# Delta blocks laid out row first and loaded in 12 transfers a group, output weights emitted with the last score row, a shared closing addition

## The chip, the cores and the metric

The kernel runs on one core of a Trainium2 chip. The core has a matrix engine (TensorE, PE in the profile; its weight loads are PEld), a vector engine (DVE), an activation engine (ACT), a general engine (GpSimd, POOL) and a sync engine (SP) that here mostly issues DMAs. Each works through its own instructions in order; semaphores tie them together. The metric is the device time of one execution in microseconds (us).

## The reference

One layer of a hybrid encoder in float32, 1024 positions, width 1024. Cut to what matters:

```python
u = rms_norm(h, mix_norm_gain)
proj = u @ w_in                                   # q,k,v of attention; q,k,v, gate, decay, beta of the delta rule
o_att = rms_norm(chunked_rel_attention(aq, ak, av), att_out_gain)      # own chunk of 64 + 8 chunks back, 8 heads
dq, dk, dv = split(causal_short_conv(dqkv), 3)    # convolution of 4 taps, then silu
o_dn = rms_norm(gated_delta_rule(dq, dk, dv, log_decay, beta), dn_out_gain) * silu(dgate)    # 4 heads of 128
h = h + concat([o_att, o_dn]) @ w_out
h = h + square(relu(rms_norm(h, ffn_norm_gain) @ w_ff1)) @ w_ff2       # 1024 -> 4096 -> 1024
```

Inside the delta rule each chunk and head needs a triangular solve:

```python
a_strict = where(strict, einsum('bhnid,bhnjd->bhnij', k_beta, k) * l_mask, 0.0)
t_mat = a_strict + eye(CHUNK)
value = triangular_solve(t_mat, v_beta, lower=True, unit_diagonal=True)
k_cumdecay = triangular_solve(t_mat, k_beta * exp(decay)[..., None], lower=True, unit_diagonal=True)
```

## The kernel before

Everything is kept feature first, so products contract over the 128 partitions. Each float32 operand is split into a high half (a cast on ACT, line 203) and a low half (a subtraction, line 204), and a product is three matrix multiplications (`mm3`, line 222): hi·lo, hi·hi, lo·hi. A scheduler lays out the instructions of each engine when the program is built, from the order in which the code emits them, their dependencies and its own model of costs; `high_priority` lifts a piece ahead.

The stages:
1. Norm and input projections (`aq_ps`, `ak_ps`, `av_ps`, `dq_ps`, `dv_ps`, `g_ps`).
2. In the shadow of the projections, `delta_prep`: for each of 8 chunks of 128 rows and 4 heads it makes the strictly lower matrix A, 128x128, and stores it to `a_dr` in DRAM (line 577). The 32x32 diagonal blocks of all chunks and heads, 128 of them, are loaded one to a partition (`ad`, line 587), inverted by 31 steps on DVE (lines 595 and 596) into `xd`, transposed back into `ad`, and both are stored as `x_dr` and `y_dr` (line 604).
3. `delta_low(b)`, once for each of two groups of four chunks: it loads the inverted blocks into `l_w` (line 630, from `y_dr`), and the blocks `l_xa` (line 633 from `x_dr`, line 634 from `a_dr`), then joins them by 32x32 matrix products into `l_p` (lines 640 and 649) to inverses of 64x64. `delta_merge` (line 658) joins these to 128x128, with `m_sa` and `m_yb`, just before a chunk needs them.
4. Attention and the delta recurrence, interleaved by a planner that keeps a clock of engines and PSUM banks: score rows `t_sa`, `t_sb` (line 925), softmax pieces `t_pa`, `t_pb` (DVE lines 945 and 956, ACT lines 964 and 968), flips (transposes) on PE into `t_tpa`, `t_tpb` (lines 985 and 1001) with copies to `t_ta`, `t_tb`, values `t_o` (line 1024), and the outputs `mixa` and `mixd` (attention half and delta half). The names with `c_` belong to the delta recurrence (`c_att`, `c_po`, `c_pq`).
5. `out_proj`: `weights(j)` loads eight 128x512 pieces of the output weights (`wo_4` to `wo_7`, then `wo_0` to `wo_3`) through `load_w`, where `wr`, the landing place, has three slots. The low half goes to POOL and DVE by turns. `mixed(hf)` splits the outputs into `mh` and `ml`, and `rows` multiplies: `op` tiles of 128x512, 24 products each. The first of these rows are emitted between the last flips of attention, three `op` tiles side by side; each adds the residual into `h` (DVE, line 1223).
6. The feed-forward, seven products a step after Strassen and Winograd (`q` tiles at line 1343, `p` tiles at line 1439). After the last product the partial results `y` are merged, subtracted from (line 1566) and stored: `y[5]` through ACT's queue (line 1464), `y[4]` through SP's (line 1567).

All DMAs of stages 2 to 4 that the change touches are issued by SP, one after another. PSUM has 8 banks; the mixer's pools hold 3 (`ps_a`, projections), 2 (`ps_t`), 1 (`ps_o`) and 2 (`ps_d`, delta) in that order, and the feed-forward opens its own four tiles of two banks over all of them.

Of the kernel before, what the change touches and what calls it, by code (L numbers as in the profile page):

```python
# [43 lines left out]
NV = 6  # L44
# [54 lines left out]
def hymba_kernel(  # L99
# [31 lines left out]
    mpool = mixer.enter_context(tc.tile_pool(name="mpool", bufs=1))  # L131
    ps_a = mixer.enter_context(tc.tile_pool(name="ps_a", bufs=3, space=PS))
    ps_t = mixer.enter_context(tc.tile_pool(name="ps_t", bufs=2, space=PS))
    ps_o = mixer.enter_context(tc.tile_pool(name="ps_o", bufs=1, space=PS))
    ps_d = mixer.enter_context(tc.tile_pool(name="ps_d", bufs=2, space=PS))

    def page(tag, name, dt=F32, w=512):
# [69 lines left out]

    def load_w(src, name, tags=("wh", "wl")):
        raw = page("wr", name + "_r")
        nc.sync.dma_start(out=raw, in_=src)  # L210
        hi = page(tags[0], name + "_h", F32R)
        lo = page(tags[1], name + "_l", F32R)
        lo_turn[0] += 1
        split(raw, hi, lo, nc.scalar, nc.gpsimd if lo_turn[0] % 2 else nc.vector)
        return hi, lo
# [77 lines left out]
    dg_dr = dram.tile([NT, P, 4, P], F32, name="dg_dr")  # L293
    a_dr = dram.tile([NT, P, 512], F32, name="a_dr")
    x_dr = dram.tile([NT * 4, 32, 4, 32], F32, name="x_dr")
    y_dr = dram.tile([NT * 4, 32, 4, 32], F32, name="y_dr")
    kt_dr = dram.tile([NT, P, 512], F32, name="kt_dr")
# [248 lines left out]
    def delta_prep(kT, ab):  # L546
# [4 lines left out]
        for c in range(NT):  # L551
            n = f"d{c}"
            h4 = slice(4 * c, 4 * c + 4)
            tp = bank(ps_d, n + "_tp")
            four_t(tp, head(kT[c]))
            ss = sumsq(page("pp", n + "_sq"), "p", tp, n)
            if c + 1 < NT:
                kt = page("pp", n + "_kt")
                nc.vector.tensor_tensor(b4(kt), b4(tp), bc_row(ab["edec"][:, 1, h4]), ALU.mult)
                nc.sync.dma_start(out=kt_dr[c], in_=kt)  # L560
            yield 500
            L = decay("pp", n + "_L", ab, h4, tri_s, tri_ur, nc.vector)
            r = rsqrt("p", ss, 4, 1.0, EPS, n)
            br, br2 = ab["br"][:, h4], ab["br2"][:, h4]
            nc.gpsimd.tensor_tensor(br, ab["beta"][:, h4], r, ALU.mult)
            nc.gpsimd.tensor_tensor(br2, br, r, ALU.mult)
            nc.gpsimd.tensor_tensor(ab["nbr"][:, h4], br2, ab["ned"][:, h4], ALU.mult)
            yield 500
            mp = bank(ps_d, n + "_m")
            four(mp, lambda h, hs: kT[c][:, hs], lambda h, hs: kT[c][:, hs])  # L570
            A = page("pp", n + "_A")
            for h in range(4):
                hs = slice(h * P, (h + 1) * P)
                nc.vector.scalar_tensor_tensor(
                    A[:, hs], mp[:, hs], ab["br2"][:, 4 * c + h:4 * c + h + 1], L[:, hs],
                    ALU.mult, ALU.mult)
            nc.sync.dma_start(out=a_dr[c], in_=A)
            yield 900
# [3 lines left out]
        td = page("pp", "td")  # L582
        for c in range(NT):
            for b in range(4):
                bs = slice(32 * b, 32 * b + 32)
                p0 = 16 * c + 4 * b
                nc.sync.dma_start(out=ad[p0:p0 + 4],
                                  in_=a_dr[c].rearrange("r (h e) -> h r e", h=4)[:, bs, bs])
        nc.gpsimd.memset(xf, 0.0)
# [12 lines left out]
        for dst, src in ((x_dr, xd), (y_dr, ad)):  # L602
            for h in range(4):
                nc.sync.dma_start(out=dst[:, :, h, :], in_=src.rearrange("(q h) r e -> h q r e", h=4)[h])

# [11 lines left out]
    def delta_low(b, W, tag):  # L617
# [5 lines left out]
        Y = [w.rearrange("p (c h e) -> p c h e", c=2, h=4) for w in W[-2:]]  # L623
        a4 = a_dr[4 * b:4 * b + 4].rearrange("c r (h e) -> c r h e", h=4)
        for i in range(2):
            nc.gpsimd.memset(W[-2 + i], 0.0)
        for c in range(4):
            q = 16 * b + 4 * c
            for k in range(4):
                nc.sync.dma_start(out=Y[c // 2][32 * k:32 * k + 32, c % 2, :, 32 * (k % 2):32 * (k % 2) + 32],  # L630
                                  in_=y_dr[q + k])
            for r0 in (0, 64):
                nc.sync.dma_start(out=XA[r0:r0 + 32, c], in_=x_dr[q + r0 // 32])
                nc.sync.dma_start(out=XA[r0 + 32:r0 + 64, c], in_=a4[c, r0 + 32:r0 + 64, :, r0:r0 + 32])
        yield clock.now + 8000, "d"
# [22 lines left out]
    def delta_merge(c, W, res):  # L658
# [5 lines left out]
        Yd = W[c // 2].rearrange("p (c h e) -> p c h e", c=2, h=4)[:, c % 2]  # L664
        nc.sync.dma_start(out=A[64:128], in_=a_dr[c].rearrange("r (h e) -> r h e", h=4)[64:128, :, 0:64])
        nc.gpsimd.memset(Y[64:128, :, 0:64], 0.0)
# [161 lines left out]

    def attention(after, delta, values, outputs):

# [266 lines left out]
        while True:  # L1097
# [69 lines left out]
            elif k == "score":  # L1167
                g, t, pp = units[begun]
                score(g, t, pp)
                begun += 1  # L1170
                if pp and begun + 2 < len(units):
                    start(*units[begun + 2][0:2])
                if pp and not g:
                    load_rest(t + 1)
            elif k == "values":
                if next(values, None) is None:
                    values_left = False
                else:
# [7 lines left out]
    def out_proj(result):


        order = (4, 5, 6, 7, 0, 1, 2, 3)
        w, parts, R, begun = [], [], {}, []  # L1190

        def weights(j):
            w.append([None] * NKT)
            for k in order:
                w[j][k] = load_w(w_out[k * P:(k + 1) * P, j * 512:(j + 1) * 512], f"wo{j}_{k}",
                                 (("wh", "u"), ("u", "wl"))[j])

# [217 lines left out]
    def ff2(psw, pools):  # L1415
# [52 lines left out]
        for kb in range(nb):  # L1468
# [198 lines left out]
```

## Time and profile before

| | |
|---|---|
| median of 3 runs | 1276.42 us (1275.62 to 1279.3) |
| profiled execution | 1273.11 us, span 1271.0 us |
| mean granted clock of PE over the span | 0.995 |
| busy: PE, DVE, ACT, POOL | 1241.2, 926.5, 547.6, 289.8 us |

The span is what the profiler saw from the first instruction to the last. In lines of the timeline the columns are the start in us, the length in us, the engine, the line of the code, the operation, what it writes and reads, how many instructions are put together, and, in brackets, how long the engine had been idle before it and what released it (`issue` where the profile names nothing). `SPq` and `ACTq` are the DMA-issuing parts of SP and ACT. In a table of windows the columns are length, busy time of PE, PEld, DVE, ACT and POOL with counts, the clock granted to PE as a share of full speed, the busy share of the core's 16 DMA engines, and what they moved in GB/s.

### The profile page before, as it was taken

To read this page: it belongs to the slowest core of one execution; us is meant where nothing else is said; L and a number is where in the kernel's file an instruction comes from. 1 tells how busy PE (TensorE), PEld (TensorE's weight loads), DVE (VectorE), ACT (ScalarE), POOL (GpSimd) and SP (SyncE) were. 2 spreads that over 40 slices of the span, in tenths; PEclk is the share of its full clock that TensorE was granted. 3 is DMA by queue.
4 is the path that set the end of the run, shared out by engine and by line. 5 is a ranking of instruction groups with operands and counts; after the bars stand their busy time and mean duration, and the time that the engine had idled before them with its cause. 6 is when DMAs were issued, how large, how long until landed. Compare 5 with 4: busy or idle time off the path is not lost.

```text
span 1271.0 us, 18018 instructions
## 1 busy us (share of the span) xinstructions
PE 1241.2 (98%) x6686; PEld 1033.3 (81%) x6686; DVE 926.5 (73%) x1388; ACT 547.6 (43%) x899; POOL 289.8 (23%) x487
## 2 busy tenths in 40 slices
PE   9999999999998999889999999999999999999998
PEld 8778878778888898778878788888887888888886
DVE  7899987654236577774349777677669997997988
ACT  7323132232245665654445454544445543333331
POOL 4425461344132345543210000000000000000034
PEclk9999999999999999989999999999999999999999
DMA  7214353564585532134441333332259623332002
GB/s 226 67 42 139 101 157 107 121 162 118 175 245 150 162 109 71 40 109 133 141 141 67 116 133 117 132 100 96 86 199 368 211 83 112 121 100 94 7 34 99
DMA packets 135398, 158.53 MB, mean 125 GB/s; under 512 B 31760, under 2 KB 79376, under 8 KB 134800
## 3 DMA queue, kind: packets, MB, share of 16 engines
q1 hardware_dynamic: 117216, 135.11, 35.0%
q10 hardware_dynamic: 18096, 22.29, 5.2%
q8 instruction: 52, 0.85, 0.3%
q14 instruction: 34, 0.28, 0.1%
HBM read 109.91 MB, written 47.45 MB: 124 GB/s over the span
## 4 chain that ended last, share of the span: by engine, by line
PE 51%; DVE 8%; issue 2%; ACT 1%; POOLq 1%; POOL 0%; DVEq 0%; ACTq 0%
PE p L1439 21%; PE q L1343 20%; PE op L222 6%; PE t_o L1024 1%; POOLq L1662 1%; DVE ml L204 1%; DVE h L1285 1%; DVE y L1511 0%; PE t_sa L925 0%; DVE q_0a_l L204 0%; DVE y L1507 0%; PE t_tpb L985 0%; DVE p43b_l L204 0%; DVE p73b_l L204 0%; DVE p43a_l L204 0%
## 5 line engine op out<-in xcount | busy, mean ns | idle before, releaser
L1511 POOL TENSOR_TENSOR y<-y,y 128x1024 f32<-128x1024 f32 x6 | 19.3, 3242 | 590.5 <-DVE y L1507 571.6
L1507 DVE TENSOR_TENSOR y<-y,p 128x1024 f32<-128x1024 f32 x46 | 55.1, 1216 | 5.4 <-PE p L1439 4.5
L222 PE MATMUL op<-mh,wo_l 128*128 128x512 f32 x128 | 50.1, 399 | 1.1 <-POOL wo_l L204 1.1
L222 PE MATMUL op<-mh,wo_h 128*128 128x512 f32 x128 | 50.6, 398 | 0.1
L222 PE MATMUL op<-ml,wo_h 128*128 128x512 f32 x128 | 50.2, 395 | 0.0
L945 DVE CUSTOM_DVE_ANT_0 t_pb<-t_sb,biasn 128x256 f32<-128x256 f32 (+1 forms) x64 | 23.2, 401 | 29.8 <-PE t_sb L925 29.8
L964 ACT ACTIVATE t_pb<-t_pb,t_nm 128x256 f32<-128x256 f32 (+1 forms) x64 | 31.4, 491 | 18.1 <-DVE t_nm L956 16.7
L1223 DVE TENSOR_TENSOR h<-op,op_x 128x512 f32<-128x512 f32 x16 | 10.8, 687 | 28.8 <-PE op L222 28.8
L1230 POOL TENSOR_TENSOR op_q<-op_q 128x512 f32<-128x512 f32 x14 | 19.6, 1397 | 47.3 <-ACT op_q L1229 47.2
L222 PEld LDWEIGHTS op<-mh,wo_l 128*128 128x128 f32 x128 | 24.4, 191 | 6.9 <-POOL wo_l L204 1.5
L222 PEld LDWEIGHTS op<-mh,wo_h 128*128 128x128 f32 x128 | 24.4, 191 | 5.9 <-issue 0.5
L222 PEld LDWEIGHTS op<-ml,wo_h 128*128 128x128 f32 x128 | 24.4, 190 | 5.2
L956 DVE CUSTOM_DVE_ANT_0 t_pa<-t_sa,biaso,t_nm 128x384 f32<-128x384 f32 (+2 forms) x48 | 25.0, 543 | 2.3 <-PE t_sa L925 2.0
L222 PE MATMUL g_ps<-uh,wg_h 128*128 128x512 f32 x64 | 25.3, 396 | 1.2 <-ACT wg_h L203 1.2
L968 ACT ACTIVATE t_pa<-t_pa,t_nm 128x384 f32<-128x384 f32 (+2 forms) x48 | 26.4, 550 | 0.0
L222 PE MATMUL aq_ps<-waq_h,uh 128*128 128x512 f32 x64 | 25.4, 400 | 0.8 <-ACT waq_h L203 0.8
L925 PE MATMUL t_sb<-ks,t_q 128*128 128x256 f32 (+1 forms) x144 | 24.0, 294 | 1.7 <-DVE t_nm L945 1.3
L222 PE MATMUL g_ps<-uh,wg_l 128*128 128x512 f32 x64 | 25.2, 393 | 0.4 <-POOL wg_l L204 0.4
L222 PE MATMUL dq_ps<-uh,wdq_h 128*128 128x512 f32 x64 | 25.5, 398 | 0.0
L222 PE MATMUL dv_ps<-uh,wdv_l 128*128 128x512 f32 x64 | 25.4, 397 | 0.0
L222 PE MATMUL dq_ps<-ul,wdq_h 128*128 128x512 f32 x64 | 25.3, 395 | 0.0
L222 PE MATMUL av_ps<-wav_l,uh 128*128 128x512 f32 x64 | 25.2, 394 | 0.0
(1109 smaller groups left out, 4306.7 us busy)
## 6 DMA issues: line engine op xcount, KB each, us to landing
wa<-in_w_ff_dram SPq DMA_DIRECT2D x32, 512.0 KB
a<-in_w_ff_dram SPq DMA_DIRECT2D x32, 512.0 KB
b<-f_dr SPq DMA_DIRECT2D x32, 512.0 KB
f_dr<-yy ACTq DMA_DIRECT2D x16, 512.0 KB
t_q<-q_dr SPq DMA_DIRECT2D x30, 256.0 KB
f_dr<-zz ACTq DMA_DIRECT2D x13, 512.0 KB
ks<-k_dr SPq DMA_DIRECT2D x16, 256.0 KB
wo_r<-in_w_out_dram SPq DMA_DIRECT2D x16, 256.0 KB
```

What stands on the lines that cost most here:

```text
L204: return a.ins, lo_eng.tensor_tensor(lo, src, hi.bitcast(F32), ALU.subtract).ins
L222: nc.tensor.matmul(ps, a, b, start=(first and i == 0), stop=(last and i == n - 1))
L925: nc.tensor.matmul(o, q[m][:, i * P:(i + 1) * P], k[:, c], start=(m == 0), stop=(m == 1))
L945: nc.vector.tensor_tensor_reduce(sb[:, c], bk[:, c], new[g][pp][:, c], -1.0, 3.0e38, ALU.add, ALU.min, nm[:, 4 + i:5 + i])
L956: nc.vector.tensor_tensor_reduce(sa[e][:, 0:wa], bk[:, 0:wa], old[g][i][:, 384 - wa:384], -1.0, nm[:, 4 + i:5 + i], ALU.add, ALU.min, nm[: ...
L964: nc.scalar.activation(sb[:, c], sb[:, c], AF.Exp, bias=m, scale=-1.0, accum_out=T["sums"][:, 4 + i:5 + i])
L968: nc.scalar.activation(sa[e][:, 0:wa], sa[e][:, 0:wa], AF.Exp, bias=m, scale=-1.0, accum_out=T["sums"][:, i:i + 1])
L1230: nc.gpsimd.tensor_tensor(acc, acc, sq, ALU.add)
L1343: nc.tensor.matmul(part(ps, q), l[:, s], r, start=(k + m == 0), stop=(k == 3 and m == 2))
L1439: nc.tensor.matmul(part(ps[q], 0) if by_rows else part(ps[q // 2], q % 2), l[:, s], part(r, k), start=(i + k + m == 0), stop=(i + k + m == 4))
L1507: nc.vector.tensor_tensor(y[i][m], y[i][m], ps[m], op)
L1511: eng.tensor_tensor(y[i][m], y[i][m], y[z][m], ALU.add)
```

## The change

Four edits in one:
1. `a_dr`, `x_dr` and `y_dr` lie with the row first in DRAM, then chunk, head and column. So one DMA can take 32 rows of several chunks at once: the loads of the diagonal blocks are 16 (two chunks each) and not 32, and a group of `delta_low` loads by 12 DMAs (two from `x_dr`, two from `a_dr`, eight from `y_dr`) and not 32, for the same bytes. Blocks now stand on partition 32·b + 4·c + h.
2. The first half of the output weights is emitted, with high priority, as soon as the last score row has been emitted, and not when the output projection begins; and all sixteen low halves of output weights are made by DVE.
3. The PSUM pool `ps_a` is made last, so the pools lie in other banks.
4. Of the closing addition `y[5] += y[7]`, one half stays on POOL, the other goes to DVE.

```diff
-    ps_a = mixer.enter_context(tc.tile_pool(name="ps_a", bufs=3, space=PS))
     ps_t = ...
     ps_o = ...
     ps_d = ...
+    ps_a = mixer.enter_context(tc.tile_pool(name="ps_a", bufs=3, space=PS))
...
-    def load_w(src, name, tags=("wh", "wl")):
+    def load_w(src, name, tags=("wh", "wl"), low=None):
...
-        split(raw, hi, lo, nc.scalar, nc.gpsimd if lo_turn[0] % 2 else nc.vector)
+        split(raw, hi, lo, nc.scalar, low or (nc.gpsimd if lo_turn[0] % 2 else nc.vector))
...
-    a_dr = dram.tile([NT, P, 512], F32, name="a_dr")
-    x_dr = dram.tile([NT * 4, 32, 4, 32], F32, name="x_dr")
-    y_dr = dram.tile([NT * 4, 32, 4, 32], F32, name="y_dr")
+    a_dr = dram.tile([P, NT, 512], F32, name="a_dr")
+    x_dr = dram.tile([32, NT * 4, 4, 32], F32, name="x_dr")
+    y_dr = dram.tile([32, NT * 4, 4, 32], F32, name="y_dr")
...
-        for c in range(NT):
+        for c in range(0, NT, 2):
             for b in range(4):
                 bs = slice(32 * b, 32 * b + 32)
-                p0 = 16 * c + 4 * b
-                nc.sync.dma_start(out=ad[p0:p0 + 4],
-                                  in_=a_dr[c].rearrange("r (h e) -> h r e", h=4)[:, bs, bs])
+                p0 = 4 * (NT * b + c)
+                nc.sync.dma_start(out=ad[p0:p0 + 8],
+                                  in_=a_dr[:, c:c + 2].rearrange("r c (h e) -> (c h) r e", h=4)[:, bs, bs])
...
         for dst, src in ((x_dr, xd), (y_dr, ad)):
-            for h in range(4):
-                nc.sync.dma_start(out=dst[:, :, h, :], in_=src.rearrange("(q h) r e -> h q r e", h=4)[h])
+            for p0 in range(0, P, 32):
+                nc.sync.dma_start(out=dst.rearrange("r q h e -> (q h) r e")[p0:p0 + 32], in_=src[p0:p0 + 32])
...
-        for c in range(4):
-            q = 16 * b + 4 * c
+        for r in range(2):
+            q = 2 * r * NT + 4 * b
+            nc.sync.dma_start(out=XA[64 * r:64 * r + 32], in_=x_dr[:, q:q + 4])
+            nc.sync.dma_start(out=XA[64 * r + 32:64 * r + 64],
+                              in_=a4[64 * r + 32:64 * r + 64, :, :, 64 * r:64 * r + 32])
+        for i in range(2):
             for k in range(4):
-                nc.sync.dma_start(out=Y[c // 2][32 * k:32 * k + 32, c % 2, :, 32 * (k % 2):32 * (k % 2) + 32],
-                                  in_=y_dr[q + k])
-            for r0 in (0, 64):
-                nc.sync.dma_start(out=XA[r0:r0 + 32, c], in_=x_dr[q + r0 // 32])
-                nc.sync.dma_start(out=XA[r0 + 32:r0 + 64, c], in_=a4[c, r0 + 32:r0 + 64, :, r0:r0 + 32])
+                q = k * NT + 4 * b + 2 * i
+                nc.sync.dma_start(out=Y[i][32 * k:32 * k + 32, :, :, 32 * (k % 2):32 * (k % 2) + 32],
+                                  in_=y_dr[:, q:q + 2])
...
                 begun += 1
+                if begun == len(units):
+                    with tc.high_priority():
+                        weights()
...
-                merge(nc.gpsimd, 5, 7)
+                for m, eng in enumerate((nc.gpsimd, nc.vector)):
+                    eng.tensor_tensor(y[5][m], y[5][m], y[7][m], ALU.add)
```

The order of the instructions as built shows what moves. SP's queue, the loads of the second group (`l_w` and `l_xa`), among loads for attention (`t_q`, `ks`, `vt`) and recurrence (`c_...`). Before, the last stretch of it:

```order
L665 DMA m_sa<-a_dr 64x4x64
L210 DMA wo_4_r<-in_w_out_dram 128x512
L700 DMA c_jq<-dq_dr 128x512
L210 DMA wo_5_r<-in_w_out_dram 128x512
L210 DMA wo_6_r<-in_w_out_dram 128x512
L905 DMA t_q<-q_dr 64x2x512 x2
L633 DMA l_xa<-x_dr 32x128
L634 DMA l_xa<-a_dr 32x4x32
L858 DMA ks_3991<-k_dr 128x512
L858 DMA ks_3993<-k_dr 128x512
L633 DMA l_xa<-x_dr 32x128
L703 DMA c_kt<-kt_dr 128x512
```

After, the same place:

```order
L635 DMA l_w_4199<-y_dr 32x8x32 x4
L667 DMA m_sa<-a_dr 64x4x64
L907 DMA t_q<-q_dr 64x2x512
L210 DMA wo_6_r<-in_w_out_dram 128x512
L907 DMA t_q<-q_dr 64x2x512
L702 DMA c_jq<-dq_dr 128x512
L907 DMA t_q<-q_dr 64x2x512 x2
L629 DMA l_xa<-x_dr 32x512
L630 DMA l_xa<-a_dr 32x16x32
L860 DMA ks_3955<-k_dr 128x512
L860 DMA ks_3957<-k_dr 128x512
L629 DMA l_xa<-x_dr 32x512
```

Before, 13 more loads of `l_xa` follow the last row shown; after, only `c_kt` and one load of `l_xa` from `a_dr`. Ahead of it 16 loads of `l_w` have become 8.

DVE at the start of the output projection, from the last softmax piece on (`wo_k_l` are low halves of weights, `ml` low halves of the mixed outputs). Before:

```order
L956 ISA t_nm 128x1
L807 SCALAR_TENSOR_TENSOR mixd_6009<-c_tpo,dng,c_jg 128x4x128
L780 TENSOR_TENSOR c_att<-c_mt,c_Lt 128x512
L1051 TENSOR_TENSOR t_on<-t_on,t_tot 128x256
L204 TENSOR_TENSOR ml_6651<-mixd_4680,mh_6650 128x512
L786 TENSOR_TENSOR c_o<-c_o,c_po 128x512
L204 TENSOR_TENSOR ml_6655<-mixd_4680,mh_6654 128x512
```

After:

```order
L958 ISA t_nm 128x1
L204 TENSOR_TENSOR wo_4_l<-wo_4_r,wo_4_h 128x512
L204 TENSOR_TENSOR wo_5_l<-wo_5_r,wo_5_h 128x512
L204 TENSOR_TENSOR wo_6_l<-wo_6_r,wo_6_h 128x512
L809 SCALAR_TENSOR_TENSOR mixd_5953<-c_tpo,dng,c_jg 128x4x128
L782 TENSOR_TENSOR c_att<-c_mt,c_Lt 128x512
L1053 TENSOR_TENSOR t_on<-t_on,t_tot 128x256
L204 TENSOR_TENSOR ml_6595<-mixd_4624,mh_6594 128x512
```

Three low halves now stand ahead of `mixd` and `c_att`; before, `wo_5_l` was the first on DVE, 12 rows behind the last one shown, and `wo_4_l` and `wo_6_l` stood on POOL. The other five low halves follow among the `ml` rows, and on ACT the casts of `wo_7` to `wo_3` stand ahead of the last four copies of flips, where before they stood behind all of them.

PE at the same place. Before, `op` products stop after six, and five pieces of attention follow:

```order
L516 MATMUL c_po<-c_vn,c_att 128x128 x4
L222 MATMUL op_6685<-mh_6650,wo_4_h 128x512
L222 MATMUL op_6742<-mh_6650,wo_4_h 128x512
L222 MATMUL op_6785<-mh_6650,wo_4_h 128x512
L222 MATMUL op_6685<-ml_6651,wo_4_h 128x512
L222 MATMUL op_6742<-ml_6651,wo_4_h 128x512
L222 MATMUL op_6785<-ml_6651,wo_4_h 128x512
L1001 MATMUL t_tpa_6521<-ident,t_pa_6334 128x128 x3
L985 MATMUL t_tpb_6533<-ident,t_pb_6403 128x128 x4
L1001 MATMUL t_tpa_6540<-ident,t_pa_6415 128x128 x3
L1001 MATMUL t_tpa_6546<-ident,t_pa_6422 128x128 x3
```

After, three products stand ahead of `c_po`, and behind it they go on in blocks of nine:

```order
L222 MATMUL op_6629<-mh_6594,wo_4_h 128x512
L222 MATMUL op_6686<-mh_6594,wo_4_h 128x512
L222 MATMUL op_6729<-mh_6594,wo_4_h 128x512
L516 MATMUL c_po<-c_vn,c_att 128x128 x4
L222 MATMUL op_6629<-ml_6595,wo_4_h 128x512
L222 MATMUL op_6629<-mh_6594,wo_4_l 128x512
L222 MATMUL op_6629<-mh_6598,wo_5_h 128x512
L222 MATMUL op_6686<-ml_6595,wo_4_h 128x512
L222 MATMUL op_6686<-mh_6594,wo_4_l 128x512
L222 MATMUL op_6686<-mh_6598,wo_5_h 128x512
L222 MATMUL op_6729<-ml_6595,wo_4_h 128x512
L222 MATMUL op_6729<-mh_6594,wo_4_l 128x512
```

After the first block of nine comes one flip, after three more the others, and the last products with values (`t_o`) stand later still.

In the first group the first `l_p` products stand, on PE, 38 products of `ak_ps` and one flip (`ak_tp`) earlier than before.

More of the change, by code (lines that the diff above doesn't have):

```diff
@@ L576, in delta_prep @@
                     ALU.mult, ALU.mult)
-            nc.sync.dma_start(out=a_dr[c], in_=A)
+            nc.sync.dma_start(out=a_dr[:, c], in_=A)
             yield 900
@@ L623, in delta_low @@
         Y = [w.rearrange("p (c h e) -> p c h e", c=2, h=4) for w in W[-2:]]
-        a4 = a_dr[4 * b:4 * b + 4].rearrange("c r (h e) -> c r h e", h=4)
+        a4 = a_dr[:, 4 * b:4 * b + 4].rearrange("r c (h e) -> r c h e", h=4)
         for i in range(2):
             nc.gpsimd.memset(W[-2 + i], 0.0)
-        for c in range(4):
-            q = 16 * b + 4 * c
-            for k in range(4):
-                nc.sync.dma_start(out=Y[c // 2][32 * k:32 * k + 32, c % 2, :, 32 * (k % 2):32 * (k % 2) + 32],
-                                  in_=y_dr[q + k])
-            for r0 in (0, 64):
-                nc.sync.dma_start(out=XA[r0:r0 + 32, c], in_=x_dr[q + r0 // 32])
-                nc.sync.dma_start(out=XA[r0 + 32:r0 + 64, c], in_=a4[c, r0 + 32:r0 + 64, :, r0:r0 + 32])
+        for r in range(2):
[4 more added lines that the diff above has]
+        for i in range(2):
+            for k in range(4):
+                q = k * NT + 4 * b + 2 * i
+                nc.sync.dma_start(out=Y[i][32 * k:32 * k + 32, :, :, 32 * (k % 2):32 * (k % 2) + 32],
+                                  in_=y_dr[:, q:q + 2])
         yield clock.now + 8000, "d"
@@ L664, in delta_merge @@
         Yd = W[c // 2].rearrange("p (c h e) -> p c h e", c=2, h=4)[:, c % 2]
-        nc.sync.dma_start(out=A[64:128], in_=a_dr[c].rearrange("r (h e) -> r h e", h=4)[64:128, :, 0:64])
+        nc.sync.dma_start(out=A[64:128], in_=a_dr[:, c].rearrange("r (h e) -> r h e", h=4)[64:128, :, 0:64])
         nc.gpsimd.memset(Y[64:128, :, 0:64], 0.0)
@@ L827, in delta_all, with attention @@
             yield gens
-    def attention(after, delta, values, outputs):
+    def attention(after, delta, values, weights, outputs):
         def bias_page(tag, name):
@@ L1184, in attention, with out_weights, out_proj @@
         return outputs_gen or outputs()
[L1186 to L1196, printed above, removed]
+    order = (4, 5, 6, 7, 0, 1, 2, 3)
+    def out_weights(w, j):
+        w.append([None] * NKT)
+        for k in order:
+            w[j][k] = load_w(w_out[k * P:(k + 1) * P, j * 512:(j + 1) * 512], f"wo{j}_{k}",
+                             (("wh", "u"), ("u", "wl"))[j], nc.vector)
+    def out_proj(result, w):
+        parts, R, begun = [], {}, []
         def mixed(hf):
@@ L1234, in rows @@
             return acc
-        weights(0)
         mixed(0)
         acc = yield from rows(0, 0, None)
-        weights(1)
+        out_weights(w, 1)
         acc = yield from rows(1, 0, acc)
@@ L1604, in hymba_kernel @@
     ab = ab_proj(u)
-    W, result = [], {}
+    W, w_o, result = [], [], {}
     after = []
@@ L1612, in hymba_kernel @@
     clock.reset()
-    rest = attention(after[NV - 1], delta_all(ab, kT, W), values, lambda: out_proj(result))
+    rest = attention(after[NV - 1], delta_all(ab, kT, W), values,
+                     lambda: out_weights(w_o, 0), lambda: out_proj(result, w_o))
     for _ in rest or ():
```

## The prediction

> **What bounds the kernel now.** I read the busy shares and the chain first, then TensorE's idle time, then its granted clock in the windows where that idle time lies.
>
> ```profile
> span 1271.0 us, 18018 instructions
> PE 1241.2 (98%) x6686; PEld 1033.3 (81%) x6686; DVE 926.5 (73%) x1388; ACT 547.6 (43%) x899; POOL 289.8 (23%) x487
> PE 51%; DVE 8%; issue 2%; ACT 1%; POOLq 1%; POOL 0%; DVEq 0%; ACTq 0%
> ```
>
> TensorE (PE) is busy for 1241.2 of 1271.0 us, and half of the chain that ended last is PE's own work, so nothing off it is worth time except where PE stands still or its clock falls. About 30 us of idle time (1271.0 - 1241.2) is all there is. The change removes no matmul, so it can win only in such places. These windows (columns: length, PE, PEld, DVE, ACT, POOL busy, granted clock, DMA share, GB/s) show the two where the clock falls to half, and one of low activity where it does not:
>
> ```profile
> 401.80:405.20 3.40, 0.66 (x21) 0.69 (x22) 1.60 (x8) 0.00 (x0) 0.82 (x4) 1.00 0.14 27
> 405.20:408.60 3.40, 3.40 (x30) 3.34 (x27) 0.00 (x0) 2.03 (x6) 0.00 (x0) 0.50 0.86 229
> 517.87:521.28 3.41, 1.92 (x15) 1.69 (x15) 2.49 (x9) 1.42 (x4) 2.70 (x8) 1.00 0.00 0
> 548.60:552.00 3.40, 1.56 (x11) 0.84 (x9) 2.47 (x4) 3.40 (x8) 1.90 (x5) 1.00 0.00 0
> 552.00:555.40 3.40, 1.76 (x7) 1.22 (x7) 3.40 (x9) 0.98 (x3) 2.79 (x5) 0.50 0.00 0
> 555.40:558.80 3.40, 3.24 (x8) 2.59 (x9) 1.28 (x3) 0.62 (x1) 3.17 (x5) 0.50 0.60 178
> 545.70:566.00 20.30, 16.41 (x101) 12.78 (x100) 13.45 (x22) 10.65 (x23) 11.49 (x18) 0.83 0.40 130
> ```
>
> A window with PE busy 19% (0.66 of 3.40) and one with 46% (1.56) were each followed by half clock; 56% (1.92) was not. So a stall costs its idle time and, if it is dense enough, half of the busy time after it.
>
> **Second group's loads (term A).** SP's queue and PE around 400 us (start, length, engine):
>
> ```profile
> 378.29 5.05 SPq L630 DMA_DIRECT2D l_w<-y_dr  x8
> 402.34 0.54 SPq L634 DMA_DIRECT2D l_xa<-a_dr  x1
> 404.55 1.44 PE L640 MATMUL l_p<-l_w,l_xa 32*32 32x32 f32 x32 [3.63 <-issue]
> ```
>
> SP issues these small loads one behind another, 5.05 us for 8 (0.63 each), while the DMA engines are at a 0.14 share: the bound is the issuing. The matmul at 404.55 begins 2.2 us after the issue at 402.34, the last load of a_dr but one, and no releaser is named, which fits a load. The change has 20 fewer issues there: 20 x 0.6 = 12 us earlier, more than the 3.63 us needed, even if a load of twice or eight times the bytes takes longer in flight. The order leaves l_p where it stood on PE. Saved: 3.63 idle, and half of the 3.40 busy us at half clock, 1.7; together 5.3. What is late next is ACT's and DVE's flips, which idled through the stall and now have less lead, so I give 0.5 back: **-4.8**, ends -3.6 (the clock falls all the same) and -5.3.
>
> **Start of the output projection (term B).** Four of PE's five waits (a fifth, between the second and third, is like them), and who ends them:
>
> ```profile
> 546.08 1.16 PE L516 MATMUL c_po<-c_vn,c_att 128*128 128x128 f32 x8 [0.24 <-DVE c_att L780]
> 549.74 0.66 PE L985 MATMUL t_tpb<-ident,t_pb 128*128 128x128 f32 x4 [0.78 <-ACT t_on L1056]
> 552.66 0.90 PE L1001 MATMUL t_tpa<-ident,t_pa 128*128 128x128 f32 x3 [0.97 <-ACT t_tb L991]
> 555.56 0.80 PE L222 MATMUL op<-mh,wo_l 128*128 128x512 f32 x1 [1.14 <-POOL wo_l L204]
> 553.92 3.28 POOL L204 TENSOR_TENSOR wo_l<-wo_r,wo_h 128x512 fp32r<-128x512 f32 x2
> 555.54 6.13 SPq L210 DMA_DIRECT2D wo_r<-in_w_out_dram  x5
> 558.12 0.62 ACT L203 CAST wo_h<-wo_r 128x512 fp32r<-128x512 f32 x1 [5.14 <-DMA wo_r<-in_w_out_dram]
> ```
>
> The five waits are 3.89 us (20.30 - 16.41). Half clock covers 1.76 + 3.24 = 5.0 busy us, so 2.5 are lost: 3.89 + 2.5 = 6.4. The cause is the low halves of the first weights: POOL reaches them at 553.92, and until then no slot comes free for the next weights, whose load then takes 2.6 us (555.54 to 558.12). Afterwards DVE makes all eight, the first three before mixd and c_att, and PE gets blocks of nine products between the last flips. The price, by these rows:
>
> ```profile
> 545.34 0.69 DVE L780 TENSOR_TENSOR c_att<-c_mt,c_Lt 128x512 f32<-128x512 f32 x1
> 554.84 1.22 DVE L204 TENSOR_TENSOR wo_l<-wo_r,wo_h 128x512 fp32r<-128x512 f32 x1
> 558.77 0.69 DVE L204 TENSOR_TENSOR wo_l<-wo_r,wo_h 128x512 fp32r<-128x512 f32 x1 [2.12 <-ACT wo_h L203]
> 543.56 0.94 SPq L1315 DMA_DIRECT2D wa<-in_w_ff_dram  x2
> 603.65 44.20 PE op L222 x192
> ```
>
> Three low halves at 0.69 (alone; 1.22 beside POOL, which is free then) put c_att 2.1 us later; PE now has one block of three products (0.7 us) ahead of c_po, whose own wait was 0.24: it waits up to 2.1 + 0.2 - 0.7 = 1.6, or less where mh holds that block. Next on ACT the casts of wo_2 and wo_3 stand ahead of the flips' copies and of mh for the attention half. Walking the chain (free slot at 545, load 2.6 and a little more, because the two loads of feed-forward weights issued at 543.56 are under way, cast, low half, next load 2.6, cast) puts wo_3's cast at about 554 and the first attention mh at 555.8. PE meanwhile has four k of nine products, 36 x 0.23 us (44.20/192) = 8.3 us, which carry it to about 558. So this second wait is covered; without that cover it would be 2 to 3 us. Left over, between 0 and 1.6 us, I take 0.9; that leaves PE busy for over 70% of its window, so the clock should hold: 0.9 - 6.4 = **-5.5**, ends -3 (1.6 of waits and one window at half clock, 1.7, remain) and -6.4 (no wait remains).
>
> The Trainium skill (TensorE: Matmul & The Clock Gate, Part 1, "What's actually happening") says that half clock comes after an idle window of about 3.4 us, on a free-running window of 3413 ns. The trace agrees on the length (405.20 to 408.60) but not on idleness: before 552.0 PE was 46% busy and none of the quoted waits reached 1.2 us. By the page the fall at 552 would have another cause and stay; that is a rival below.
>
> **PSUM pool order (term C).** The first product of the feed-forward waits for the bank that h's addition (DVE, L1223) frees:
>
> ```profile
> 648.71 0.47 PE L1343 MATMUL q<-b11h,q_0a_h 128*128 128x512 f32 x1 [0.88 <-DVE h L1223]
> 660.00:708.00 48.00, 47.91 (x229) 39.90 (x228) 48.00 (x44) 29.29 (x29) 0.00 (x0) 1.00 0.24 81
> ```
>
> With ps_a last, those banks are others and long free: at most -0.88. But DVE is busy for 48.00 of 48.00 us just after, and what PE gains it will mostly wait for there: **-0.3**, ends -0.9 and 0.
>
> **Closing addition (term D).** The last rows of DVE, POOL and the two store queues, and the DMA engines after:
>
> ```profile
> 1258.02 4.62 DVE L1511 TENSOR_TENSOR y<-y,y 128x1024 f32<-128x1024 f32 x4
> 1262.56 1.87 DVE L1566 TENSOR_TENSOR y<-y,p 128x512 f32<-128x512 f32 x3
> 1265.88 0.69 DVE L1566 TENSOR_TENSOR y<-y,p 128x512 f32<-128x512 f32 x1 [1.44 <-PE p L1439]
> 1259.38 7.84 POOL L1511 TENSOR_TENSOR y<-y,y 128x1024 f32<-128x1024 f32 x2 [13.70 <-DVE y L1511]
> 1263.27 3.66 SPq L1567 DMA_DIRECT2D out_dram<-y  x4
> 1264.93 2.70 ACTq L1464 DMA_DIRECT2D out_dram<-y  x2
> 1264.50:1269.50 5.00, 1.34 (x6) 0.76 (x5) 0.69 (x1) 0.00 (x0) 2.72 (x2) 0.93 1.01 381
> ```
>
> POOL's 7.84 us look like the end, but the DMA engines are full from 1264.5 to 1269.5 (share 1.01): the last 2 MB are bound by their volume, so the end is set by when the first store starts. That was SP's at 1263.27. DVE now does one half of y5 += y7 ahead of the three subtractions (4.62/4 = 1.15 us), so the first subtraction and SP's first store come 1.15 later, and POOL's own half is not ready sooner (ACT's first store came at 1264.93). The 1.44 us of DVE idle cover the last subtraction only. So **+1.0**, ends -0.9 (if the transfers catch up and the second POOL half was the last) and +1.2.
>
> **First group (term E).** SP's stores and loads, and PE:
>
> ```profile
> 234.12 2.73 SPq L604 DMA_DIRECT2D x_dr<-xd  x3
> 244.94 0.63 SPq L604 DMA_DIRECT2D y_dr<-ad  x1
> 247.75 5.07 SPq L630 DMA_DIRECT2D l_w<-y_dr  x8
> 261.96 1.19 PE L640 MATMUL l_p<-l_w,l_xa 32*32 32x32 f32 x32
> 271.11 0.73 PE L222 MATMUL aq_ps<-waq_h,uh 128*128 128x512 f32 x2 [0.84 <-ACT waq_h L203]
> 234.00:246.00 12.00, 12.00 (x58) 9.85 (x57) 7.33 (x21) 2.34 (x4) 4.40 (x6) 1.00 0.91 161
> ```
>
> Ten loads, not 24, remain behind the stores; but the order also puts l_p some 38 products of 0.23 us (about 9 us) earlier on PE, at about 252.8. Eight l_w loads from 247.75 at 0.63 are issued by 252.8, and the needed ones land 0 to 1.7 us after l_p's turn. Against it, the weights behind them on SP come earlier, and the wait of 0.84 at 271.11 should go. **+0.4**, ends -0.8 and +2. The loads for the solve fall to 16 and DVE waits for the last four as before: nothing.
>
> **Sum.** -4.8 - 5.5 - 0.3 + 1.0 + 0.4 = -9.2. The profiled execution took 1273.11 us (2.1 around its span), 3.3 below the median of 1276.42; it would take 1263.9, and the median 1267.2. A difference under 0.3% (3.8 us) can't be told from none.
>
> **Rivals.** *The projection's gain is given back* (B = 0): ACT works in order, and if the casts of wo_2 and wo_3 come 3 us later than I walked, its copies and mh hold PE for as long as before, and the clock falls again. For it: ACT stood 5.14 us for that load at 558.12. Against: 8.3 us of products lie ready. -3.7: 1272.7. *The clock at 552 falls for another reason* (the page's rule): 2.5 us of B stay, 1269.7. Against it speak the two quoted windows of 19% and 46%. *The wait at 404.55 ended on something else than a load*: no releaser is named; A = 0, 1272.0. *Slower: the first group's stores.* x_dr and y_dr are written in pieces of 128 bytes, 16 KB apart afterwards, and the DMA share was already 0.91 over 234 to 246. Were the 11.4 us of stores twice as long, l_p would wait 11.4 us more, with some 2.5 of clock loss: -9.2 + 13.9 = +4.7, 1281.1. From 1.6 times on the gain is gone, from 1.9 it is slower by over 0.3%. Against it: the pieces and their number are the same.
>
> **How the numbers follow.** Forecast 0.62; gain given back 0.15 (at 1272.7, on the bound: half faster, half same); clock 0.08 (faster); not a load 0.06 (0.04 faster, 0.02 same); stores 0.07 (0.05 slower, 0.02 same); others, such as several small waits, 0.02 same. Faster 0.82, same 0.13, slower 0.05. The low end is the sum of the lower ends, -5.3 - 6.4 - 0.9 - 0.9 - 0.8 = -14.3, 1262; the upper end takes in the given-back gain with its spread, 1274.
>
> **What would show it.** A: l_p's matmul near 400 without a wait, clock 1.0 through 400 to 412. B: waits under 2 us in the 20 us from the first op product, clock 1.0; if wrong, a wait on mh or c_att in that place. C: no wait at the first q. D: SP's first closing store later, the DMA engines full to the end. E: a wait of under 2 us at the first l_p; over 5 us would make the prediction wrong, as would half clock anywhere new.

## The result, and the profile after

The changed kernel takes 1264.76 us (median of 4 runs, 1264.33 to 1267.61) against 1276.02 us of the kernel before, run beside it (4 runs, 1272.14 to 1279.3): a ratio of 0.9911, 95% interval 0.9884 to 0.9938, 11.3 us faster. The profiled executions are 1264.75 and 1273.11 us: 8.4 us apart. The page of the kernel after:

```profile
span 1263.0 us, 17948 instructions
PE 1238.2 (98%) x6686; PEld 1030.9 (82%) x6686; DVE 930.4 (74%) x1397; ACT 547.2 (43%) x899; POOL 278.4 (22%) x478
PEclk9999999999999999999999999999999999999999
```

PE does the same 6686 products in 3.0 us less busy time (1241.2 to 1238.2): that is time no longer spent at half clock, and no slice of the clock row is below 9. The rest of the 8.0 us of span is idle time.

The two places, in windows and in PE's timeline:

```profile
400.00:412.00 12.00, 11.65 (x179) 10.63 (x178) 9.12 (x30) 6.52 (x19) 2.73 (x9) 1.00 0.31 90
545.00:566.00 21.00, 20.79 (x117) 16.74 (x118) 15.03 (x27) 11.10 (x22) 6.76 (x15) 1.00 0.40 126
391.08 1.08 PE L927 MATMUL t_sb<-ks,t_q 128*128 128x128 f32 x8 [1.18 <-DVE c_o L790]
403.47 1.19 PE L642 MATMUL l_p<-l_w,l_xa 32*32 32x32 f32 x32
544.25 0.96 PE L222 MATMUL op<-mh,wo_h 128*128 128x512 f32 x3 [0.81 <-ACT mh L203]
545.14 1.16 PE L516 MATMUL c_po<-c_vn,c_att 128*128 128x128 f32 x8
639.44 0.39 PE L1348 MATMUL q<-b11h,q_0a_h 128*128 128x512 f32 x1
```

`l_p` begins without a wait, and the clock is 1.00 in both windows. A smaller wait is new at 391.08 (1.18 us). At the output projection PE idles 0.2 us in 21, after a wait of 0.81 for the first `mh`; the wait for `c_att` that DVE's three low halves might have made did not come. The first `q` product has no wait. The end of the kernel:

```profile
1253.22 1.21 DVE L1564 TENSOR_TENSOR y<-y,y 128x1024 f32<-128x1024 f32 x1
1254.35 1.87 DVE L1572 TENSOR_TENSOR y<-y,p 128x512 f32<-128x512 f32 x3
1250.03 6.66 POOL L1564 TENSOR_TENSOR y<-y,y 128x1024 f32<-128x1024 f32 x1 [13.70 <-DVE y L1516]
1255.06 2.52 SPq L1573 DMA_DIRECT2D out_dram<-y  x4
1256.72 0.94 ACTq L1469 DMA_DIRECT2D out_dram<-y  x2
1256.11 0.39 PE L1444 MATMUL p<-p43b_h,p43a_l 128*128 128x512 f32 x1
1257.50:1261.50 4.00, 0.00 (x0) 0.00 (x0) 0.00 (x0) 0.00 (x0) 0.00 (x0) 0.77 0.99 375
```

POOL's one half now takes 6.66 us, beside a DVE that never pauses, and SP's first closing store is issued 1.05 us before PE's last product begins; before it was 2.2 us ahead of it:

```profile
1265.45 0.39 PE L1439 MATMUL p<-p43b_h,p43a_l 128*128 128x512 f32 x1
```

From that product to the end of the span it is 6.9 us now (1263.0 - 1256.11) and was 5.55 (1271.0 - 1265.45).

Followed along PE from one marked product to the next, the difference of the two profiles is made up so: to the first product of `ak_ps` +0.9; from there to the first `t_sb` +0.8; to the last of the second group's first products (`l_p`, line 640 before, 642 after) -4.3, the wait and its half clock; to the last `op` product -5.6; to the first `q` -1.1; to PE's end 0; to the end of the span +1.3. Together -8.0. The first +0.9 is no clear cost: over all kernels here the first `ak_ps` starts between 214.6 and 216.3 us, with no order between old loads and new.

### The profile page after: what moved, and what is told of

Same layout as the page of the kernel before. It is cut to its first block, busy times and chain, and to the rows that moved or that the text cites. A ratio compares the mean times of both kernels' runs of the same rounds, so it can differ in the third digit from the quotient of the medians.

```text
span 1263.0 us, 17948 instructions
## 1 busy us (share of the span) xinstructions
PE 1238.2 (98%) x6686; PEld 1030.9 (82%) x6686; DVE 930.4 (74%) x1397; ACT 547.2 (43%) x899; POOL 278.4 (22%) x478
## 4 chain that ended last, share of the span: by engine, by line
PE 54%; DVE 6%; ACT 1%; issue 1%; DMA 1%; POOL 0%; DVEq 0%; ACTq 0%; SPq 0%
PE p L1444 23%; PE q L1348 20%; PE op L222 6%; PE t_o L1026 1%; DMA wo_r<-in_w_out_dram 1%; DVE h L1290 1%; PE t_sa L927 0%; DVE q_0a_l L204 0%; PE t_tpb L987 0%; PE t_sb L927 0%; PE c_pv L516 0%; PE t_tpa L1003 0%; PE t_tpo L520 0%; PE c_pq L516 0%; DVE t_pa L958 0%
## 5 line engine op out<-in xcount | busy, mean ns | idle before, releaser
L1516 POOL TENSOR_TENSOR y<-y,y 128x1024 f32<-128x1024 f32 x4 | 11.5, 2899 | 575.6 <-DVE y L1512 570.8
L222 PE MATMUL aq_ps<-waq_l,uh 128*128 128x512 f32 x64 | 25.3, 395 | 0.0
```

What stands on the lines that cost most here:

```text
L222: nc.tensor.matmul(ps, a, b, start=(first and i == 0), stop=(last and i == n - 1))
```

## The experiments

**The loads alone.** Every edit on `a_dr`, `x_dr` and `y_dr` in the kernel before, nothing else. They change three things at once: the layout, the number of loads, and their order. Before, a group loads chunk by chunk, and the first `l_p` starts with the last chunk; after, it loads one block row of all chunks first, the one that the first `l_p` needs.

```diff
-    a_dr = dram.tile([NT, P, 512], F32, name="a_dr")
+    a_dr = dram.tile([P, NT, 512], F32, name="a_dr")
...
+            nc.sync.dma_start(out=XA[64 * r:64 * r + 32], in_=x_dr[:, q:q + 4])
```

> The kernel before with the row-first layout and its 16 + 12 + 12 loads alone. Theory (the second group's loads were late because SP issues them one by one): l_p's wait of 3.6 us near 400 is gone and the clock stays at 1.0 there, -4.4 us; the first group and what follows cost +0.8; together -3.6, near 1272.5 for a before of 1276. The half clock near 552 stays. Rival (the wait at l_p ended on something other than a load): the 3.6 us stay, time 1276 or, with the first group's cost, 1277.

Measured: 0.9975 (0.9962 to 0.9987), 1270.9 against 1273.89 us. `l_p` has no wait, the clock holds there, and the half clock of the output projection is still there:

```profile
402.07 1.19 PE L642 MATMUL l_p<-l_w,l_xa 32*32 32x32 f32 x32
550.00:555.00 5.00, 3.84 (x11) 2.90 (x12) 3.34 (x6) 0.18 (x1) 4.83 (x5) 0.50 0.32 100
```

So the wait did end on a load. From the first `ak_ps` to the first `t_sb` of attention it is 144.8 us, against 143.0 to 144.2 in the kernels here with the old loads of the first group: the first group's cost.

**The weights alone.** The edits on `load_w`, `out_weights` and their call.

```diff
+                if begun == len(units):
+                    with tc.high_priority():
+                        weights()
...
-                                 (("wh", "u"), ("u", "wl"))[j])
+                             (("wh", "u"), ("u", "wl"))[j], nc.vector)
```

> The kernel before with the early output weights and all their low halves on DVE alone. Theory (the first weights' low halves held PE up, and the thin stretch brought the clock down): waits of about 1 us and full clock from 545 to 566, -5.6 us, near 1270.5; the wait of 3.6 us near 400 and the half clock behind it stay. Rival (the clock fell at 552 for another reason, since PE had no idle window): half clock near 552 again, about -3, near 1273. Rival (given back on ACT): no change.

Measured: 0.9936 (0.992 to 0.9952), 1265.93 us. Full clock throughout, at the output projection as expected, and near 400 as not expected:

```profile
550.00:555.00 5.00, 4.61 (x21) 3.46 (x19) 4.05 (x9) 2.93 (x7) 1.48 (x3) 1.00 0.49 152
390.51 1.08 PE L925 MATMUL t_sb<-ks,t_q 128*128 128x128 f32 x8 [2.47 <-DMA t_q<-q_dr]
402.91 1.19 PE L640 MATMUL l_p<-l_w,l_xa 32*32 32x32 f32 x32
386.42:389.84 3.42, 1.63 (x15) 1.43 (x13) 2.36 (x8) 2.76 (x11) 0.00 (x0) 1.00 0.65 141
```

The early emission also moved SP's queue: a load of output weights now stands between the two loads of queries for a score row, and the second of these is issued at 384.87 us (384.02 before). PE waits 2.47 us for the queries 12 us ahead of `l_p`, and by then the `l_xa` loads are there. The delay was paid at another matmul, more cheaply, because this wait did not bring the clock down. That was close: in the window that holds most of the wait PE was busy 48% (1.63 of 3.42), and 46% was followed by half clock in the kernel before. So the two parts overlap near 400. Their ratios multiply to that of the change (0.9975 x 0.9936 = 0.9911), but by the profiles the loads save little on top of the weights: the span is 1264.0 us with the weights alone and 1263.0 with all four edits, of which the PSUM order gives 1.1 and the closing addition costs 1.3 (the next two experiments), so some 1.2 us are left for the loads.

**The PSUM order alone**, read in the profile.

```diff
-    ps_a = mixer.enter_context(tc.tile_pool(name="ps_a", bufs=3, space=PS))
...
+    ps_a = mixer.enter_context(tc.tile_pool(name="ps_a", bufs=3, space=PS))
```

> The kernel before with the PSUM pool order changed alone; read in the profile. Theory (the first product of the feed-forward waits for a bank and the gain is kept): no wait at the first q, and the distance from the last op product to the first p product is 1.0 us shorter than in the kernel before. Rival (DVE, busy throughout afterwards, takes it back, as the prediction took it): the distance is shorter by 0.3 or less.

Measured: one run, 1274.34 us. The first `q` has no wait. By the rows of tiles (count, durations in ns, first and last start), from the last `op` product to the first of the `p` stage, in this kernel and then in the one before:

```profile
L222 PE MATMUL op<-mh,wo_l x128: 388/389/796, 557.0 to 649.7; 128*128 128x512 f32 x128
L1439 PE MATMUL p<-p10b_h,p10a_h x16: 389/389/389, 955.2 to 970.4; 128*128 128x512 f32 x16
```

```profile
L222 PE MATMUL op<-mh,wo_l x128: 388/389/797, 555.6 to 647.4; 128*128 128x512 f32 x128
L1439 PE MATMUL p<-p10b_h,p10a_h x16: 389/389/389, 954.0 to 969.2; 128*128 128x512 f32 x16
```

305.5 against 306.6: the 1.1 us are kept. The saturated DVE takes nothing back. One profile is enough here: the other kernels with the old order of pools have 306.5 or 306.6, those with the new one 305.4 or 305.5.

**The closing addition alone**, read in the profile.

```diff
-                merge(nc.gpsimd, 5, 7)
+                for m, eng in enumerate((nc.gpsimd, nc.vector)):
+                    eng.tensor_tensor(y[5][m], y[5][m], y[7][m], ALU.add)
```

> The kernel before with the closing addition shared between POOL and DVE alone; read in the profile. Theory (the last 2 MB are bound by the DMA engines, so the first store sets the end, and DVE's half delays it by 1.15): from PE's last product to the end of the span 6.4 us, against 5.2 before. Rival (POOL's 7.84 us set the end): 4.3 us.

Measured: one run, 1282.32 us.

```profile
span 1280.5 us, 18017 instructions
1273.66 0.39 PE L1439 MATMUL p<-p43b_h,p43a_l 128*128 128x512 f32 x1
```

6.84 us from the start of PE's last product to the end (6.45 from its end, where 6.4 was expected), as in the changed kernel: this part costs 1.3 us. The rest of the single time arose ahead of the closing stage: PE's last product starts 8.2 us later than in the profiled kernel before, and PE was busy 6.0 us longer (1247.2 against 1241.2), with a granted clock of 0.991 against 0.995. Near 560 half clock lasted 6.8 us, as before. Near 406 it lasted 10.24 us, where the profiled kernel before had 3.4, and it came a third time near 980:

```profile
406.40:416.64 10.24, 9.47 (x104) 9.15 (x106) 1.73 (x5) 3.80 (x11) 0.00 (x0) 0.50 0.50 140
979.84:983.26 3.42, 3.42 (x10) 2.64 (x9) 2.32 (x3) 0.50 (x1) 0.00 (x0) 0.50 1.03 408
```

**Early emission, low halves by turns.** The second experiment without the move to DVE.

```diff
-                             (("wh", "u"), ("u", "wl"))[j], nc.vector)
+                             (("wh", "u"), ("u", "wl"))[j])
```

> The weights alone again (as in the second experiment, which gave 0.9936), but with the low halves by turns on POOL and DVE as before: early emission without the move to DVE. Theory (the early low halves free the landing slots early, whichever engine makes them): most of the gain stays, ratio 0.994 to 0.996, full clock from 545 to 566. Rival (the move to DVE carries it, because POOL's low halves take 1.3 to 1.6 us and stand behind its small steps): 0.998 to 1.0, with a wait on wo_l from POOL and half clock near 552.

**Low halves on DVE, emitted late.** The other half.

```diff
-                                 (("wh", "u"), ("u", "wl"))[j])
+                                 (("wh", "u"), ("u", "wl"))[j], nc.vector)
```

> The kernel before with the low halves of all output weights on DVE, but emitted where they were. Theory (early emission carries the gain): the low halves still stand behind the mixed outputs' on DVE, so the wait before the first product with a low half stays and the clock falls: 0.998 to 1.001. Rival (the move to DVE carries it): 0.994 to 0.996.

Measured: early by turns 0.9938 (0.9916 to 0.996); DVE but late 0.9986 (0.9969 to 1.0004). The early one first, then the late one:

```profile
550.00:555.00 5.00, 4.78 (x25) 3.69 (x24) 2.50 (x4) 2.16 (x6) 4.75 (x7) 1.00 0.53 157
```

```profile
555.03 0.55 PE L1001 MATMUL t_tpa<-ident,t_pa 128*128 128x128 f32 x3 [0.97 <-ACT t_tb L991]
555.00:560.00 5.00, 3.83 (x33) 3.39 (x35) 4.96 (x12) 0.35 (x1) 3.96 (x8) 0.73 0.20 55
```

The place in the order carries the gain, not the engine: late on DVE keeps the wait for the flips' copies (0.97) and half clock.

**The changed kernel, second group split into 32 loads again.**

```diff
+            for c in range(4 if b else 0):
+                nc.sync.dma_start(out=XA[64 * r:64 * r + 32, c:c + 1], in_=x_dr[:, q + c:q + c + 1])
...
```

> The changed kernel, with the second group's loads split again into 32 of 16 KB, from the row-first layout. Theory (the number of issues on SP was the bound): about 20 issues of 0.6 us come back, and with them a wait of 2 to 4 us on a load between 385 and 405, either at l_p or, as in the second experiment, at a score row that waits for its queries; 1.5 to 5 us slower than the changed kernel, near 1267. Rival (the layout itself made the loads faster): no wait on a load there, the same time as the changed kernel, 1264.8.

Measured: 0.9914 (0.9889 to 0.9939), 1264.58 us: no slower, and `l_p` waits for nothing. That went against the theory. Most of the loads of `l_xa` took 0.42 to 0.43 us of SP each, not 0.58, and all blocks that the first `l_p` needs stood ahead of the others; the last of them is the first row here:

```profile
395.46 0.42 SPq L631 DMA_DIRECT2D l_xa<-a_dr  x1
401.27 1.19 PE L649 MATMUL l_p<-l_w,l_xa 32*32 32x32 f32 x32
```

Both could explain it, so the next kernel takes the layout with the old count and the old order.

**The layout alone, 32 loads in the old order.**

```diff
+                nc.sync.dma_start(out=Y[c // 2][32 * k:32 * k + 32, c % 2:c % 2 + 1, :, 32 * (k % 2):32 * (k % 2) + 32],
+                                  in_=y_dr[:, k * NT + q:k * NT + q + 1])
...
```

> The kernel before with the row-first layout, but with each group's loads as 32 of 16 KB, in the order of before. Theory A (the number of issues is the bound): as in the kernel before, a wait of 3 to 4 us at l_p near 400 and half clock behind it, ratio near 1.000. Theory B (the layout makes each issue shorter, 0.43 us where it was 0.58, as the loads that were split again showed, so 32 loads come 5 us earlier): no wait at l_p, ratio near 0.9975 as with the loads alone.

Measured: 0.9973 (0.9954 to 0.9992).

```profile
399.14 0.42 SPq L634 DMA_DIRECT2D l_xa<-a_dr  x1
401.07 1.32 PE L640 MATMUL l_p<-l_w,l_xa 32*32 32x32 f32 x32 [1.51 <-issue]
398.48:401.89 3.41, 1.90 (x36) 1.74 (x35) 2.98 (x9) 0.58 (x2) 2.43 (x8) 1.00 0.23 49
401.89:405.30 3.41, 3.41 (x25) 3.32 (x22) 0.16 (x2) 2.03 (x6) 0.00 (x0) 0.50 0.95 249
```

Between the theories: the shorter issues bring the load that `l_p` needs 3.2 us earlier (399.14 against 402.34), the wait shrinks from 3.63 to 1.51, and the clock still falls. So the layout is about half of the cure for the wait. The other half is the order or the number of the loads. By these rows the order would be enough (an estimate): with as many loads, the kernel with the second group split again issues the load that `l_p` needs at 395.46, another 3.7 us earlier. That is 4.1 us ahead of the time at which `l_p` would begin here without its wait (401.07 - 1.51 = 399.56), and it needed 1.9 us from issue to use. Fewer loads bring it to 388.43 in the changed kernel. No run here has fewer loads in the old order, so what the number does by itself is not shown. In time the two kernels, 0.9973 and 0.9975, can't be told apart.

**A probe of the clock and of SP's issues.**

```diff
+    dense(90)
+    for g, n in ((8, 11), (6, 13), (5, 14), (4, 16), (3, 18), (2, 20), (1, 22)):
+        thin(g, n)
+        dense(90)
...
+    for k in range(N):
+        nc.sync.dma_start(out=land(k, 0)[0:32, 0], in_=old[k])
...
```

> No layer is computed here; the output is zeros. TensorE runs dense stretches of 90 products and between them, for some 20 us each, groups of 8, 6, 5, 4, 3, 2 and 1 products that wait for a copy on ScalarE; SyncE issues loads of 32 rows, 16 of a kind one after another. On the clock: if a low busy share brings it down (the 46% and 19% windows of the kernel before), it falls to half in the stretches with small groups, somewhere between 46% and 56% busy, and stays full with large ones; rival (only a whole idle window brings it down): full clock in all of them, since no gap is over 1.5 us. On the issues: if the layout sets their length, 16 KB from one contiguous block take 0.55 to 0.6 us each and 16 KB of 32 rows 16 KB apart 0.42; if the place in the kernel set it, both take the same. A load of 64 KB takes under twice the 16 KB one.

Windows of 3.41 us of the probe: among groups of three products; ahead of the fall among groups of two, and behind it; ahead of the fall among single products; then, at the end of the groups of two, one partly and one wholly in the dense stretch, and the return:

```profile
254.61:258.03 3.42, 1.96 (x8) 0.97 (x7) 0.00 (x0) 1.17 (x2) 0.00 (x0) 1.00 0.00 0
283.63:287.04 3.41, 1.52 (x5) 0.60 (x4) 0.00 (x0) 1.51 (x3) 0.00 (x0) 1.00 0.00 0
287.04:290.45 3.41, 2.38 (x4) 1.00 (x4) 0.00 (x0) 0.83 (x2) 0.00 (x0) 0.50 0.00 0
341.68:345.09 3.41, 1.65 (x5) 0.56 (x4) 0.00 (x0) 1.49 (x3) 0.00 (x0) 1.00 0.00 0
317.80:321.20 3.40, 2.67 (x7) 2.15 (x7) 0.00 (x0) 0.59 (x1) 0.00 (x0) 0.50 0.00 0
321.20:324.60 3.40, 3.40 (x9) 2.66 (x9) 0.00 (x0) 0.00 (x0) 0.00 (x0) 0.50 0.00 0
324.13:327.55 3.42, 3.42 (x15) 2.77 (x15) 0.00 (x0) 0.00 (x0) 0.00 (x0) 0.93 0.00 0
282.95 0.73 PE L153 MATMUL th<-x,lhs 128*128 128x512 f32 x2 [0.73 <-ACT x L154]
```

At 57% busy (1.96 of 3.42) the clock stayed full for 30 us. It fell after a window with PE busy 45% (1.52 of 3.41) and, among single products, after one of 48% (1.65), with no gap longer than the 0.73 of the last row. Once fallen, a window of 79% (2.67 of 3.40, at half clock) did not bring it back; a full one did. That refutes the rival of an idle window. The kernels show that the limit is not sharp in the profile's busy share: a window of 48% held in the kernel with the weights alone, and the one of 56% in the layout alone (1.90 of 3.41) was followed by half clock. Its last 0.8 us are the 32x32 products of `l_p`; whether these count for less was not tested. The issues, 16 of a kind:

```profile
26.89 7.45 SPq L165 DMA_DIRECT2D w<-old_dr  x16
34.39 7.37 SPq L167 DMA_DIRECT2D w<-new_dr  x16
41.81 7.38 SPq L169 DMA_DIRECT2D w<-new_dr  x16
49.23 10.59 SPq L171 DMA_DIRECT2D w<-olda_dr  x16
59.85 9.38 SPq L174 DMA_DIRECT2D v<-newa_dr  x16
69.28 10.17 SPq L177 DMA_DIRECT2D v<-old_dr  x16
79.50 7.98 SPq L179 DMA_DIRECT2D v<-new_dr  x16
```

In order: `x` blocks of 16 KB from one contiguous block, 0.47 us each; the same row first, 0.46; 64 KB row first, 0.46; `a` blocks of 16 KB the old way 0.66, 64 KB the new way 0.59; `y` blocks of 16 KB the old way 0.64, 32 KB the new way 0.50. Two to four times the bytes cost no more. The expectation for the `x` loads (0.55 to 0.6 against 0.42) failed here: what made them 0.58 in the kernel before is not their own shape and stays open. They alternate with `a` loads there, at 0.59 and 0.55, and that pair takes as long as the probe's 0.47 and 0.66 together; so the length may be that of the `a` loads, but no run tests it.

**The closing addition first.** In the changed kernel, all of `y[5] += y[7]` on DVE, with its stores, ahead of the additions to `y[4]`.

```diff
-                merge(nc.vector, 4, 7)
-                for m, eng in enumerate((nc.gpsimd, nc.vector)):
-                    eng.tensor_tensor(y[5][m], y[5][m], y[7][m], ALU.add)
+                merge(nc.vector, 5, 7)
                 store(y[5], 1, 1, nc.scalar)
+                merge(nc.vector, 4, 7)
```

> The changed kernel with the closing addition of y[7] to y[5] wholly on DVE and emitted, with its stores, ahead of the additions to y[4]. Theory (the last 2 MB are bound by the DMA engines from the first store on): y[5]'s 1 MB leaves up to 3 us earlier, the end is then set by the last subtraction and its store; from the start of PE's last product to the end of the span 4.5 to 5.2 us, against 6.9 in the changed kernel and 5.5 before. Rival (DVE sets the end, and gets one more addition of 1.15 us): 7 us or more.

Measured: 0.9893 (0.9873 to 0.9913), 1262.16 us, the fastest here; the changed kernel's 0.9911 lies inside the interval, so the gain over it rests on the profile:

```profile
1254.38 0.39 PE L1444 MATMUL p<-p43b_h,p43a_l 128*128 128x512 f32 x1
1250.46 2.65 ACTq L1469 DMA_DIRECT2D out_dram<-y  x2
1253.76 2.47 DVE L1571 TENSOR_TENSOR y<-y,p 128x512 f32<-128x512 f32 x4
1254.00:1258.00 4.00, 0.77 (x4) 0.31 (x2) 2.23 (x4) 0.00 (x0) 0.00 (x0) 0.84 0.94 354
```

5.1 us from PE's last product to the end (1259.5 - 1254.38), against 6.9: ACT's stores leave 4 us ahead of PE's last product, and DVE, with one more addition, does not set the end. This edit also takes the addition off POOL; a kernel that moves the stores forward and leaves POOL its half was not run.

## Why the prediction was right, point by point

- **A, second group's loads (-4.8).** -4.3 in the profile; place as written, and the wait was for a load. The cause was told too simply: it counted 20 fewer issues of 0.6 us each. But 32 loads in the new order left no wait either, and with neither order nor number changed the shorter issues took 2.1 of the 3.63 us. The new order is not in the prediction at all. What would be late next was named as the flips; it was the 1.18 at 391.08, a score row behind `c_o`. The early weights alone also end the wait at `l_p`, so with them in the kernel the loads add some 1.2 us, not 4.3; the prediction did not see that the two parts overlap.
- **B, start of the output projection (-5.5).** -5.6. The chain walked by hand held: the first `mh` was the one wait (0.81), the casts of the last weights were covered by the blocks of nine products. By the two halves, early emission carries it; the rival that the gain is given back, and the one that the clock falls for another reason, are both out.
- **The clock rule.** The prediction read a limit between 46% and 56% busy off three windows, and took over 70% as safe. The second held; the limit turned out less sharp (48% was not followed by half clock in one kernel, 56% was in another). The Trainium skill (TensorE: Matmul & The Clock Gate, Part 1, "What's actually happening") names an idle window of about 3.4 us as what brings half clock. Neither the 46% window of the kernel before nor the probe agrees with that: half clock came after windows of 45% and 48% with gaps of 0.73 us. The measurement decides.
- **C, PSUM order (-0.3).** -1.1, and this was the mis-sized step: the prediction let the saturated DVE take two thirds back, and it took nothing.
- **D, closing addition (+1.0).** +1.3. The DMA engines bind the end, and the first store sets it: SP's came 1.1 us later against PE's last product, as walked. POOL's half turned out slower than walked (6.66 us), which left ACT's stores last.
- **E, first group (+0.4).** From the first `ak_ps` to the first `t_sb` it is 144.8 to 145.0 us in the kernels with the new loads of the first group and 143.0 to 144.2 in the others: between +0.6 and +2.0. The place was wrong: `l_p`, where the prediction put the cost, had no wait at all, so the rival of slower stores is out too. PE's wait for `ak_n` grew from 1.0 to 1.7 us; why is not shown.
- **The base.** Against the profiled execution the sum gave 1263.9, and 1264.75 was measured. That it came so close is in part luck: the 0.8 us that C gave beyond its forecast make up for 0.5 missing in A and 0.3 more cost in D. The median was forecast 2.4 us too high by the step that added 3.3 us for the difference of median and profile. Much of that difference fits the first of the two places. Term A took 1.7 us for half clock near 400 from one profile, in which it lasted 3.4 us. In the three other profiles with that wait at `l_p` at 3.0 to 3.6 us (PSUM order, closing addition, low halves late) it lasted 10.24 us, with PE busy for 9.5 to 10.2 of them, and so cost some 5. The profiled execution was a mild one. The runs without a profile fit this, with clocks from 0.991 (1277.9 and 1279.6 us) to 0.996 (1271.6 us), but where the clock fell in them is not recorded. With both places gone, the median and the profiled run of the changed kernel agree (1264.76 and 1264.75). A third place is left: PE waits 1.8 us for `p50b_l` near 970, and the clock fell there in two profiles (loads alone, closing addition). The change does not touch it.

## What to carry to other kernels

On a kernel that one engine fills to 98%, look for its waits and for the windows behind them: a stretch in which PE is half busy costs its idle time and then half of what follows, and how much differs from run to run (3.4 or 10.24 us of half clock at the same place), so removing it steadies the time as well. When many small loads are late, measure what one issue takes on the queue: here it hardly depends on the bytes, so one load of four blocks took SP no longer than a load of one. Then look at which load the first product needs: together with the new layout, putting that one ahead of the others left no wait here. At the end of a kernel whose last transfers fill the DMA engines, the thing to move is the first store, not the last sum.

## What the runs showed of the hardware that was not expected

- In the probe the clock fell after windows of 3.41 us with PE busy 45% and 48%, with gaps of 0.73 us, and held at 57%. Back up, a window of 79% was not enough and a full one was; in the kernel with the closing addition alone even a full one (409.81 to 413.23) was not, and the next was.
- In one trace the changes of the clock lie whole multiples of 3.41 us apart (in the kernel before 408.61 and 551.97 us, 42 of them), and in each run they lie elsewhere against the program. So whether a stretch with few products brings half clock is in part luck: the 1.8 us wait near 970 did so in two profiles and not in the others.
- One DMA issue on SP took 0.46 us for 16 KB and for 64 KB of the same rows; loads in pieces of 128 bytes, at the source or at the target, took 0.50 to 0.66, less in the new layout than in the old.
- POOL's addition of 128x1024 took 6.66 us beside a DVE that never paused, and 7.84 for two when DVE paused; DVE's own additions beside it stayed at 1.15.
